# Moving bias rows, cache loads, cache transposes and one weight split to other places in a hybrid-attention step

## The chip, the cores and the metric

The kernel runs on one core of a Trainium2 chip. The metric is device time in microseconds (us) of one execution; lower is better. Times of the kernel before come from three runs (median 970.5 us, 969.71 to 972.78) and from one execution that was also profiled (969.89 us).

## The reference

The program is one inference step (one layer) of a streaming encoder, for a prompt of 1024 rows and a sample of 64 rows of 1024 numbers, in float32:

```
def project(x, norm_w, w_in, q_norm_w, k_norm_w):
    h = rms_norm(x, norm_w) @ w_in
    sb_q, sb_k, sb_v, sb_z, cb_q, cb_k, cb_v, cb_z, g_sb, g_cb = jnp.split(h, SPLIT_POINTS, axis=-1)
    ...
    cb_q = rms_norm(cb_q.reshape(lead + (N_HEADS_CB, HEAD_DIM)), q_norm_w)
    cb_k = rms_norm(cb_k.reshape(lead + (N_HEADS_CB, HEAD_DIM)), k_norm_w)

def merge(x, o_sb, z_sb, o_cb, z_cb, g_sb, g_cb, w_proj_sb, w_proj_cb, w_out):
    b_sb = (o_sb.reshape(lead + (WIDTH_SB,)) * jax.nn.silu(z_sb)) @ w_proj_sb
    b_cb = (o_cb.reshape(lead + (WIDTH_CB,)) * jax.nn.silu(z_cb)) @ w_proj_cb
    h = jax.nn.sigmoid(g_sb) * b_sb + jax.nn.sigmoid(g_cb) * b_cb
    return x + h @ w_out
```

Between the two stand a stick-breaking attention (sb, 8 heads of 64) and a chunk-band attention (cb, 8 heads of 64) with a bias that depends on the clipped relative position. The sample rows attend to 512 cached keys and values of each kind as well (`cache_sb_k`, `cache_cb_k`, 512 x 512 each). What matters here is the projection `x @ w_in` and what is prepared beside it for the attention: the cached keys, turned so that a head's 64 numbers lie along the partitions, and rows of the bias laid out per relative position.

## The kernel before, in words

**How the work is written.** Every engine has its own instruction stream, which it works off in order; the schedule is manual, so the order of the streams is the order of the source. A tile of a pool has a fixed number of buffers, and whoever writes a buffer again waits for its last readers. TensorE (PE in the profile) multiplies and transposes, ScalarE (ACT) and VectorE (DVE) empty its accumulators, GpSimd (POOL) subtracts and raises to powers, and SyncE (SP) issues nearly all DMAs in one queue, in order: a DMA that waits for its source or its buffer holds up all that stand behind it. Float32 products are made from two fp32r halves: `hi` is a rounded copy made on ScalarE, `lo` the difference from it, made on POOL or VectorE; one product takes three matmuls (hi x hi, lo x hi, hi x lo).

**First stage: six passes of nine tiles.** The loop `for i in range(nb)` runs over six column blocks of 256 columns of `w_in`, and within it `for ti, t in enumerate(TO)` over nine row tiles: the sample tile first (ti = 0, 64 rows, 16 matmuls), then eight prompt tiles (ti = 1 to 8, 24 matmuls each). I write (i, ti) for a place in it. After the matmuls of a place, in the order of the source:

- `post_nat` transposes an earlier tile's normalised result on PE into `pk`, which ScalarE and VectorE copy out as `hl` (lines 370 to 375). `pk` has one buffer.
- `evac_nat` empties the accumulator: ScalarE squares it (`sqn`, L340), VectorE scales and reduces it (`qn`, `msn`, L341, L343), POOL makes the reciprocal root (`rsn`, L272, L273). For the sample tile `fold` comes first, one copy on ScalarE (`fl`, L318) and one addition on VectorE (L319).
- `norm_nat` scales the tile before on ScalarE (`qn`, L352, four instructions).
- At ti = 3 and ti = 6 `W.split` makes the halves of the next pass's weights (ScalarE L131, then POOL L138 `wlo` or `wlox`), and `load_nat` issues the load of the weights of the pass after that (L123, `wraw` or `wrawx`). `wrawx` has one buffer, so its load waits for POOL's `wlox`.
- At some places `make_rb(h)` makes the bias row of head h on VectorE (`rx`, L267 and L268, two buffers) from the bias table, which sits in a tile named `ck`, and sends it to DRAM (L269).
- At eight places `next(tjobs)` adds up four pieces of x on VectorE (`d`, L189), and splits the sum of the job before into `t0h`, `t0l` and so on (ScalarE L172, VectorE L173).
- `cache_load(b)` loads one cache's keys, 1024 KB, into the tile `ck` (L386). `ck` has one buffer, shared by the bias table, the sb keys and the cb keys in turn.
- `cache_pair(b, p)` turns a quarter of them: four transposes on PE into `pc` (L392; one buffer, PSUM), a copy on ScalarE into `hc` (L394; one buffer), the difference on VectorE (L395), and a DMA of `hc` to DRAM (`d_csbT`, `d_ccbT`, L52).

Before the change `make_rb` runs at every second place from (1, 0) to (2, 5); the sb cache is loaded at (2, 6) and turned at (3, 1), (3, 3), (3, 5), (3, 7); the cb cache is loaded at (3, 7) and turned at (4, 1), (4, 3), (4, 5), (4, 7).

**Second stage: seven products.** The loop `for s in range(7)` makes the cb values of the prompt from seven products of sums of x and sums of weight blocks instead of eight. Each step s has 48 matmuls (L699), half for c = 0 and half for c = 1, and `split_quad` makes the halves of a weight sum for a later step: that of `quad[0, 0]`, which holds a difference of weight blocks, is made at s = 2 on ScalarE and VectorE (`whix` L474, `wlox` L476) and used at s = 4. The sixteen jobs of `tjobs` must be through by s = 5; the last three are called at (s, c) = (0, 0), (0, 1), (1, 0). The results gather in three banks of two: step 1 fills bank 2, step 4 adds to it, step 5 adds again. So PE may start a half of step 4 only when VectorE has read bank 2 after step 1 (`u`, L707), and a half of step 5 only when VectorE has read it after step 4 (`o`, L714). `o` has two buffers; step 3 sends two of them to DRAM (`put_v`, L635), and step 4 writes the same buffers. Ahead of those DMAs in SP's queue stand the ones of the sample's result (`fl`, L319 on VectorE, L653 to L655).

After these stages come the other columns of the projection (L863), the attention (L1032 to L1380) and the output.

Of the kernel before, what the change touches and what calls it, by code (L numbers as in the profile page):

```python
# [33 lines left out]
def hybrid_step_kernel(ctx: ExitStack, tc: tile.TileContext, x_prompt, x_sample, c_sbk, c_sbv, c_cbk, c_cbv,  # L34
# [58 lines left out]
    def pad(pool, n):  # L93
        pool.tile([128, n // 4], F32, name=f"pad{n}", bufs=1)
# [119 lines left out]
    with ExitStack() as ph:  # L214
# [49 lines left out]
        def make_rb(h):  # L264
            rb = rbs[0]
            rx = p1h.tile([128, 768], F32, name="rx", bufs=2)
            V.tensor_scalar(rx[:, 0:512], rb[:, h, 256:257].to_broadcast([128, 512]), -1.0, None, op0=OP.mult)  # L267
            V.tensor_scalar(rx[:, 512:768], rb[:, h, 255::-1], -1.0, None, op0=OP.mult)  # L268
            SP.dma_start(d_rb[h], rx)  # L269
# [259 lines left out]
        tms = [None] * 4  # L529
        jobs_at = [(2, 0), (2, 3), (2, 6), (3, 0), (3, 4), (3, 7), (4, 1), (4, 4)]  # L530

        def open_t(ns):
            tp = sx.enter_context(tc.tile_pool(name=f"tp{ns[0]}", bufs=1, side="right"))
            for n in ns:
                tms[n] = [tp.tile([128, 4, XO], F32R, name=f"t{n}{s}") for s in "hl"]
            if ns[0] == 0:
                pad(tp, 128)

        for i in range(nb):
            if i == 1:  # L540
                p0x.close()
                open_t((0, 1))
                tjobs = make_t(tms, tq)
            for ti, t in enumerate(TO):
# [28 lines left out]
                if i == 0:  # L573
                    if ti == 2:
                        load_nat(1, 0)
                        load_nat(1, 1)
                        SP.dma_start(wqk[:, 0], q_norm_w[0:1, :].to_broadcast([128, 64]))
                        SP.dma_start(wqk[:, 1], k_norm_w[0:1, :].to_broadcast([128, 64]))
                if ti in (3, 6) and i > 0 or ti in (6, 7) and i == 0:
                    h = 1 if ti == (6 if i else 7) else 0  # L580
                    if i + 1 < nb:
                        W.split((i + 1, h), V if i == 0 and h else None)
                    if i + 2 < nb:
                        load_nat(i + 2, h)
                    elif i + 2 == nb:
                        load_quad(h, 0, *((natx, "wrawx", 1) if h else (wpool, "wraw", 2)))
                if (i, ti) == (0, 4):
                    load_rb()
                if (9 * i + ti - 9) % 2 == 0 and 0 <= 9 * i + ti - 9 < 16:
                    make_rb((9 * i + ti - 9) // 2)  # L590
                if i == nb - 1 and ti == 1:
                    load_quad(0, 1, wpool, "wraw", 2)
                    load_quad(1, 1, pn, "q11", 1)
# [17 lines left out]
                    V.tensor_tensor(out=quad[0, 0], in0=quad[0, 0], in1=quad[0, 1], op=OP.subtract)  # L611
                if (i, ti) in jobs_at or i == nb - 1 and ti >= 4:
                    next(tjobs)
                if (i, ti) in ((2, 6), (3, 7)):
                    cache_load("sb" if i == 2 else "cb")
                if i in (3, 4) and ti in (1, 3, 5, 7):
                    cache_pair("sb" if i == 3 else "cb", ti // 2)
                if (i, ti) in ((1, 1), (1, 5)):
                    for s in range(2):
                        h = ti // 4  # L620
# [42 lines left out]
        for s in range(7):  # L663
# [27 lines left out]
            for c in range(2):  # L691
                if s < 3:
                    bank["1231223"[s], c] = psB.tile([128, 512], F32, name=f"b{'1231223'[s]}{c}")
                ps = bank["1231223"[s], c]
                for tt in range(2):
                    o = ps[:, 256 * tt:256 * tt + 256]
                    for k in range(4):
                        for e, (xe, w) in enumerate(((0, wh), (1, wh), (0, wl))):
                            TE.matmul(o, x(xe, k, 2 * c + tt), w[:, k], start=s < 3 and k == e == tt == 0,  # L699
                                      stop=k == 3 and e == 2, skip_group_check=True)  # L700
                two = lambda v: (v[:, 0:256], v[:, 256:512])
                if s == 0:
                    s1[c] = nu.tile([128, 512], F32, name="s1")
                    A.activation(s1[c], ps, AF.Copy)
                elif s == 1:
                    u2[c] = nu.tile([128, 512], F32, name="u2")
                    V.tensor_tensor(out=u2[c], in0=ps, in1=s1[c], op=OP.add)  # L707
                elif s == 3:
                    v = nu.tile([128, 512], F32, name="o")
                    A.activation(v, ps, AF.Copy)  # L710
                    put_v(0, 0, c, two(v))
                elif s == 4:
                    v = nu.tile([128, 512], F32, name="o")
                    V.tensor_tensor(out=v, in0=ps, in1=s1[c], op=OP.add)  # L714
                    V.tensor_tensor(out=v, in0=bank["3", c], in1=v, op=OP.add)
                    put_v(1, 1, c, two(v))
                elif s == 5:
                    V.tensor_tensor(out=s1[c], in0=ps, in1=s1[c], op=OP.add)
                    put_v(1, 0, c, two(s1[c]))
                elif s == 6:  # L720
                    V.tensor_tensor(out=u2[c], in0=ps, in1=u2[c], op=OP.add)
                    put_v(0, 1, c, two(u2[c]))
                if 2 * s + c < 3:
                    next(tjobs)
        assert not list(tjobs)

# [1066 lines left out]
```

## Time and profile before

| what | value |
|---|---|
| median of three runs | 970.5 us (969.71 to 972.78) |
| the profiled execution's own time | 969.89 us |
| its span, from the first to the last instruction | 968.1 us |
| mean granted clock of TensorE | 0.995 |
| TensorE busy | 954.5 us, 99% of the span |
| VectorE, ScalarE, POOL busy | 590.5, 500.4, 394.4 us |

All times below count from the span's start. First-stage passes 2, 3 and 4 lie between 67 and 159 us, the second stage between 181 and 228 us. The chain that ended last gives TensorE 89% of the span. A matmul's row shows the start of it and a modelled end; the distance between starts (some 0.12 us for 256 columns at full clock) is what it costs. In a timeline row the first two numbers are start and duration in us; a bracket at the end names the idle time before the instruction and what released it. In a row of windows stand, after the stretch, its length, then the busy time of PE, of the weight loads (PEld), DVE, ACT and POOL with the instructions in brackets, the granted clock of TensorE, the share of the DMA engines and GB/s.

### The profile page before, as it was taken

The page shows a single profiled execution, that of the slowest core. Times are in us where ns is not written, and L with a number is a line of the kernel's source. Part 1 is how long each engine was busy: PE and PEld are TensorE (multiplying, and loading weights), DVE is VectorE, ACT ScalarE, POOL GpSimd, SP SyncE. Part 2 cuts the span into 40 slices and gives each one's busy share as a digit, 9 for nine tenths or more (in the row PEclk, how much of TensorE's full clock was granted, in tenths as well). Part 3 has the DMA queues.
Part 4 walks back from the last instruction along what each step waited for, and adds up shares of the span by engine and source line. Part 5 has one row for each costly group of instructions (what it writes and reads, how often), then busy time and mean ns, then how long its engine had stood idle before and what let it go on. Part 6 is the DMA issues. An engine that isn't in the chain of part 4 may idle for free.

```text
span 968.1 us, 20544 instructions
## 1 busy us (share of the span) xinstructions
PE 954.5 (99%) x7595; PEld 907.2 (94%) x7595; DVE 590.5 (61%) x1156; ACT 500.4 (52%) x1159; POOL 394.4 (41%) x393
## 2 busy tenths in 40 slices
PE   9999899999999999999999999999999999999998
PEld 8999899989999999999999987788888988999998
DVE  6656564984454555534322298777777865499745
ACT  6566575332434433333342377667886874466220
POOL 3277464335444556665542200011331111686641
PEclk9999999999999999999999999999999999999999
DMA  7745666325646565555523997679799833852742
GB/s 226 245 130 195 221 223 227 111 71 192 190 142 184 171 189 169 170 173 152 179 86 103 283 244 211 161 189 250 237 296 252 243 108 89 255 176 84 219 139 75
DMA packets 173498, 175.77 MB, mean 182 GB/s; under 512 B 30922, under 2 KB 157710, under 8 KB 173271
## 3 DMA queue, kind: packets, MB, share of 16 engines
q1 hardware_dynamic: 162102, 159.58, 55.5%
q10 hardware_dynamic: 8608, 8.20, 2.7%
q0 software_dynamic: 2688, 6.69, 2.1%
q8 instruction: 60, 0.98, 0.4%
q14 instruction: 40, 0.32, 0.1%
HBM read 112.42 MB, written 62.00 MB: 180 GB/s over the span
## 4 chain that ended last, share of the span: by engine, by line
PE 89%; DVE 5%; DMA 2%; ACT 1%; issue 1%; POOL 1%; ACTq 0%; DVEq 0%; SPq 0%; POOLq 0%
PE b L863 30%; PE acc L528 13%; PE o L1380 7%; PE z L1288 7%; PE pt L1341 7%; PE b L1700 6%; PE acc L1139 5%; PE acc L1032 5%; PE b L1181 4%; PE b L699 2%; DVE d L189 2%; PE pt L301 1%; DMA ck<-in_cache_sb_k_dram 1%; DMA ck<-in_cache_cb_k_dram 1%; DVE acc L1226 1%
## 5 line engine op out<-in xcount | busy, mean ns | idle before, releaser
L1310 DVE TENSOR_TENSOR_SCAN be<-be,imp 128x128 f32<-128x128 f32 (+7 forms) x64 | 83.4, 1343 | 8.1 <-ACT be L1291 7.9
L1341 PE MATMUL pt<-ident,be 128*128 128x128 f32 (+1 forms) x568 | 87.7, 278 | 0.6 <-ACT wT L1350 0.4
L1288 PE MATMUL z<-ks,sq 128*128 128x320 f32 (+5 forms) x384 | 87.5, 338 | 0.0
L1350 ACT ACTIVATE wT<-pt 128x512 f32<-128x512 f32 (+3 forms) x123 | 57.0, 496 | 42.9 <-PE pt L1341 42.8
L1341 PEld LDWEIGHTS pt<-ident,be 128*128 128x128 f32 (+1 forms) x568 | 65.7, 140 | 13.1 <-issue 4.6
L863 PE MATMUL b<-xm,wlox 128*128 128x256 f32 (+1 forms) x336 | 76.0, 286 | 0.0
L871 DVE TENSOR_TENSOR u<-b,s 128x256 f32<-128x256 f32 (+1 forms) x56 | 24.4, 440 | 75.5 <-PE b L863 71.1
L1288 PEld LDWEIGHTS z<-ks,sq 128*128 128x128 f32 x384 | 63.7, 190 | 1.7
L1380 PE MATMUL o<-wT,vp 128*64 128x256 f32 (+1 forms) x608 | 64.2, 356 | 0.0
L1380 PEld LDWEIGHTS o<-wT,vp 128*64 128x64 f32 x608 | 40.3, 136 | 23.6 <-issue 7.5
L863 PEld LDWEIGHTS b<-xm,wlox 128*128 128x128 f32 x336 | 56.8, 188 | 0.0
L1313 ACT ACTIVATE be<-be,sm 128x640 f32<-128x640 f32 (+5 forms) x68 | 47.2, 695 | 17.2 <-DVE sm L1312 17.2
L528 PE MATMUL acc<-whi,xa 128*128 128x256 f32 x192 | 53.1, 296 | 0.0
L936 POOL DMA_DIRECT2D d_osb<-zt x20 | 10.8, 541 | 101.6 <-DVE zt L1389 55.3
L528 PE MATMUL acc<-wlo,xa 128*128 128x256 f32 x192 | 50.2, 281 | 0.0
L528 PE MATMUL acc<-whi,xm 128*128 128x256 f32 x192 | 50.2, 281 | 0.0
L528 PE MATMUL acc<-whix,xm 128*128 128x256 f32 x192 | 50.1, 280 | 0.0
L528 PE MATMUL acc<-whix,xb 128*128 128x256 f32 x192 | 50.1, 280 | 0.0
L528 PE MATMUL acc<-wlox,xm 128*128 128x256 f32 x192 | 49.9, 280 | 0.0
L1301 ACT ACTIVATE be<-be,sm 128x640 f32<-128x640 f32 (+5 forms) x68 | 47.3, 696 | 4.9 <-DVE sm L1293 4.5
L457 POOL TENSOR_TENSOR whix<-ws,whix 128x512 fp32r<-128x512 f32 x28 | 36.6, 1307 | 31.9 <-ACT whix L456 25.7
L1291 ACT ACTIVATE be<-z 128x384 f32<-128x384 f32 (+6 forms) x104 | 47.9, 515 | 3.2 <-PE z L1288 2.3
(379 smaller groups left out, 3256.6 us busy)
## 6 DMA issues: line engine op xcount, KB each, us to landing
wraw<-in_w_in_dram SPq DMA_DIRECT2D x31, 512.0 KB, 4.6
wrawx<-in_w_in_dram SPq DMA_DIRECT2D x16, 512.0 KB, 4.9
sq<-d_qsbT SPq DMA_DIRECT2D x32, 192.0 KB, 6.2
sq<-d_qcbT SPq DMA_DIRECT2D x32, 192.0 KB, 5.5
xt<-in_x_prompt_dram SPq DMA_DIRECT2D x8, 512.0 KB
d_kcbT<-hl SPq DMA_DIRECT2D x8, 512.0 KB
d_qcbT<-hl SPq DMA_DIRECT2D x8, 512.0 KB, 5.4
ks<-d_ksbT SPq DMA_DIRECT2D x16, 256.0 KB, 6.1
```

Source lines behind the costliest of these rows:

```text
L528: TE.matmul(ps, x, w, start=first, stop=last)
L863: TE.matmul(ps[:, :m], w[:, hl_, k], right[s](x)[:, k, a:b], start=s < 3 and k == 0 and e == 0, stop=k == 3 and e == 2, skip_group_check=s ...
L1032: TE.matmul(ps[:, :b - a], w[:, k], xk(x, k)[:, a:b], start=k == 0 and n == 0, stop=k == KT - 1 and n == 2)
L1139: TE.matmul(ps[:, :e - a], w[:, p, cw], g[:, a:e], start=m % 12 == 0, stop=m % 12 == 11)
L1288: TE.matmul(z[:, :m], s[:, e, q0:q0 + 128], ks[:, h, o + x:o + y], start=(e, h) == parts[0], stop=(e, h) == parts[-1])
L1291: A.activation(be[:r, x:y], z[:r, :m], AF.Sigmoid, scale=-0.125)
L1301: A.activation(be[:, :n], be[:, :n], AF.Exp, bias=kp[:, j:j + 1], scale=-1.0, accum_out=kp[:, 2:3])
L1310: V.tensor_tensor_scan(be[:r, n - 1::-1], be[:r, n - 1::-1], im[:, ::-1], 0.0, op0=OP.mult, op1=OP.max)
L1341: TE.transpose(pt[:kr, x, :r], be[:r, kb * 128:kb * 128 + kr], ident[:r, :r])
L1350: A.activation(w[:, sl:sl + m, q0:q0 + r], pt[:, :m, :r], AF.Copy)
L1380: TE.matmul(o[hd * 64:hd * 64 + 64, c0:c1], vv[:kr, kb, hd * 64:hd * 64 + 64], wT[b, p, j, hd, s // 4][:kr, s % 4, c0:c1] if j < 4 else wT ...
L1700: TE.matmul(ps[:, t], left[s](xs_, k)[:, ts_], wt_[:, k], start=s < 3 and t == k == e == 0, stop=k == 3 and e == 2, skip_group_check=s > 2 ...
```

## The change

Three things move, and no instruction is added or removed.

- Bias rows: `make_rb` runs at (1, 0), (1, 1), (1, 3), (1, 4), (1, 6), (1, 7), (2, 0), (2, 1), so the last is four places earlier than before.
- Caches: `cache_load` is called at (2, 2) for sb and (3, 2) for cb, in the source ahead of the weight loads at ti = 3 and 6. The sb keys are turned at (2, 5), (2, 7), (3, 0), (3, 1) and the cb keys at (3, 5), (3, 7), (4, 0), (4, 1).
- The last of the sixteen jobs is called at (s, c) = (2, 0) in place of (1, 0), and so stands behind the split of `quad[0, 0]`.

```
+        rb_at = [(1, 0), (1, 1), (1, 3), (1, 4), (1, 6), (1, 7), (2, 0), (2, 1)]
...
+                if ti == 2 and i in (2, 3):
+                    cache_load("sb" if i == 2 else "cb")
                 if ti in (3, 6) and i > 0 or ti in (6, 7) and i == 0:
...
-                if (9 * i + ti - 9) % 2 == 0 and 0 <= 9 * i + ti - 9 < 16:
-                    make_rb((9 * i + ti - 9) // 2)
+                if (i, ti) in rb_at:
+                    make_rb(rb_at.index((i, ti)))
...
-                if (i, ti) in ((2, 6), (3, 7)):
-                    cache_load("sb" if i == 2 else "cb")
-                if i in (3, 4) and ti in (1, 3, 5, 7):
-                    cache_pair("sb" if i == 3 else "cb", ti // 2)
+                at = [(2, 5), (2, 7), (3, 0), (3, 1)]
+                if (i, ti) in at:
+                    cache_pair("sb", at.index((i, ti)))
+                if (i - 1, ti) in at:
+                    cache_pair("cb", at.index((i - 1, ti)))
...
-                if 2 * s + c < 3:
+                if (s, c) in ((0, 0), (0, 1), (2, 0)):
                     next(tjobs)
```

What this does to the streams is seen at three places. The first is SP's queue in pass 2: `d_rb` are the bias rows, `ck` the cache load, `wraw` and `wrawx` the weight loads at ti = 3 and ti = 6, `d_csbT_78` the first turned quarter of the sb keys, `out_dram` and `d_kcbT` results of pass 2 and pass 1.

```order
-L269 DMA d_rb_131<-rx 128x768
+L269 DMA d_rb_133<-rx 128x768
+L386 DMA ck<-in_cache_sb_k_dram 128x4x512
 L52 DMA d_kcbT_74<-hl 256x1x512
 L52 DMA d_kcbT_75<-hl 256x1x512
 L123 DMA wraw<-in_w_in_dram 128x4x256
-L269 DMA d_rb_132<-rx 128x768
-L269 DMA d_rb_133<-rx 128x768
+L52 DMA d_csbT_78<-hc 128x1024
 L357 DMA out_dram<-qn 128x256
 L123 DMA wrawx<-in_w_in_dram 128x4x256
-L386 DMA ck<-in_cache_sb_k_dram 128x4x512
```

The cache load moved from behind both weight loads to ahead of both, right behind the last bias row. The second place is ScalarE at (3, 0) and (3, 1), from the sample's `fold` on, before the change:

```order
L318 ACTIVATE fl<-acc 64x256
L340 ACTIVATE sqn<-fl 64x256
L352 ACTIVATE qn<-qn,rsn 128x64 x4
L172 ACTIVATE t0h<-d 128x544
L374 ACTIVATE hl<-pk 128x2x128
L340 ACTIVATE sqn<-acc 128x256
L352 ACTIVATE qn<-qn,rsn 64x64 x4
L394 ACTIVATE hc<-pc 128x512
```

And the same place after the change, where the two rows of `hc` are the third and the fourth quarter of the sb keys (before, the one row was the first quarter):

```order
L318 ACTIVATE fl<-acc 64x256
L340 ACTIVATE sqn<-fl 64x256
L352 ACTIVATE qn<-qn,rsn 128x64 x4
L172 ACTIVATE t0h<-d 128x544
L394 ACTIVATE hc<-pc 128x512
L374 ACTIVATE hl<-pk 128x2x128
L340 ACTIVATE sqn<-acc 128x256
L352 ACTIVATE qn<-qn,rsn 64x64 x4
L394 ACTIVATE hc<-pc 128x512
```

Two quarters now follow each other one place apart, the first of them behind the sample's `fold` and a job's `t0h`. The third place is VectorE in the second stage, around the last job (`d` and `t3l`), the two reads of bank 2 after step 1 (`u`) and the split for step 4 (`wlox`):

```order
-L707 TENSOR_TENSOR u_2960<-b_2935,s_2890 128x512
+L712 TENSOR_TENSOR u_2960<-b_2935,s_2890 128x512
+L712 TENSOR_TENSOR u_2987<-b_2962,s_2923 128x512
+L476 TENSOR_TENSOR wlox<-wraw,whix 128x1024
 L189 TENSOR_TENSOR d<-xm,t1h 128x544
 L189 TENSOR_TENSOR d<-d,xb 128x544
 L189 TENSOR_TENSOR d<-d,t1l 128x544
 L173 TENSOR_TENSOR t3l<-d,t3h 128x544 x2
-L707 TENSOR_TENSOR u_2995<-b_2970,s_2923 128x512
-L476 TENSOR_TENSOR wlox<-wraw,whix 128x1024
-L673 TENSOR_TENSOR s_2758<-wrawx,s_2758 128x1024
+L678 TENSOR_TENSOR s_2758<-wrawx,s_2758 128x1024
```

The split and the second read of bank 2 moved ahead of the last job; the instructions from the first `u` to `s` are the same ones in another order. On ScalarE the split's `whix` moved ahead of the last two `t3h` likewise.

## The prediction

> **What bounds the kernel now.** I read the page first, for which engine is full, then TensorE's waits, then the windows around each wait.
>
> ```profile
> span 968.1 us, 20544 instructions
> PE 954.5 (99%) x7595; PEld 907.2 (94%) x7595; DVE 590.5 (61%) x1156; ACT 500.4 (52%) x1159; POOL 394.4 (41%) x393
> ```
>
> TensorE is full. A reordering can win only what TensorE waits, and what waiting does to its clock. The waits of TensorE, longest in total:
>
> ```profile
> PE pc L392 <- DMA ck<-in_cache_sb_k_dram: 3.2, 1, 3.2
> ...
> PE pc L392 <- DMA ck<-in_cache_cb_k_dram: 1.4, 1, 1.4
> PE b L699 <- DVE wlox L476: 1.0, 1, 1.0
> PE b L699 <- ACT whix L474: 0.9, 1, 0.9
> ```
>
> These four are what the change aims at: 3.2 + 1.4 + 1.0 + 0.9 = 6.5 us. Next, the windows that hold each wait and the ones behind them; the number to see is the granted clock, third from the end:
>
> ```profile
> 99.20:102.50 3.30, 0.66 (x6) 0.66 (x7) 2.35 (x6) 2.08 (x7) 2.21 (x4) 1.00 0.96 335
> 102.60:105.80 3.20, 3.20 (x18) 3.20 (x17) 0.69 (x1) 0.53 (x1) 0.44 (x1) 0.51 1.11 395
> 129.80:133.20 3.40, 2.33 (x20) 2.09 (x19) 2.00 (x6) 2.52 (x10) 2.00 (x3) 1.00 1.00 302
> 133.30:136.60 3.30, 3.12 (x27) 3.12 (x28) 3.23 (x7) 1.63 (x5) 2.02 (x2) 1.00 1.03 380
> 204.90:208.30 3.40, 1.52 (x11) 1.12 (x10) 3.31 (x6) 3.04 (x5) 0.46 (x1) 1.00 0.00 0
> 208.40:211.70 3.30, 3.28 (x15) 3.28 (x16) 3.30 (x2) 0.88 (x2) 2.20 (x1) 0.51 0.54 159
> ```
>
> Where TensorE worked 0.66 of 3.3 us or 1.52 of 3.4 us, the next 3.3 us ran at half clock; where it worked 2.33 of 3.4, nothing followed. So between 1.1 and 1.9 us of idleness in such a stretch the clock falls. The price is in the chain, whose rows are start, duration, what:
>
> ```profile
> 102.50 4.34 PE acc L528 x24
> 107.06 2.75 PE acc L528 x24
> ...
> 216.59 11.12 PE b L699 x96
> ```
>
> The tile after the sb wait took 4.34 us, a tile at full clock 2.75: 1.6 us lost. Two of three places paid it, so the most that can be won is 6.5 + 2 x 1.6 = 9.7 us.
>
> **The bias rows and the sb load.** SP's queue, VectorE's last two bias-row instructions at (2, 1), and TensorE after the matmuls of (2, 5), (3, 1) and (4, 1):
>
> ```profile
> 94.04 0.38 SPq L123 DMA_DIRECT2D wrawx<-in_w_in_dram  x1
> 94.47 0.50 SPq L386 DMA_DIRECT2D ck<-in_cache_sb_k_dram  x1
> 113.85 0.53 SPq L52 DMA_DIRECT2D d_csbT<-hc  x1
> 128.28 0.34 SPq L52 DMA_DIRECT2D d_csbT<-hc  x1
> 74.37 0.42 DVE L267 TENSOR_SCALAR rx<-ck 128x512 f32<-128x512 f32 x1
> 74.70 0.29 DVE L268 TENSOR_SCALAR rx<-ck 128x256 f32<-128x256 f32 x1
> 84.09 0.38 PE L370 MATMUL pk<-ident,qn 128*128 128x128 f32 x2
> 98.22 0.38 PE L370 MATMUL pk<-ident,qn 128*128 128x128 f32 x2
> 131.75 0.38 PE L370 MATMUL pk<-ident,qn 128*128 128x128 f32 x2
> ```
>
> The load was issued at 94.47, behind `wrawx`, and landed when the wait of 3.2 us ended, 98.6 + 3.2 = 101.8: 7.3 us. Now it waits only for the last bias row. At (2, 1) a row is made at 74.37 to 74.99 already; one more at (2, 0) pushes it by 0.7, to 75.7. With SP's time for the row's DMA the load goes out at about 76.3 and lands at 83.6. The first transposes can start behind `pk` at 84.09, at 84.3. That wait is gone, with 0.7 us to spare; I take 0, and up to 0.7 for the range, since a bias row may itself wait for its buffer's DMA.
>
> The eight bias rows cost VectorE what they did, 0.7 us each; two in neighbouring places delay `hl` by as much, and `pk` has its place of 3 us to cover it. Nothing on the path.
>
> **What is late next at (3, 1).** The quarters are now at (2, 5), (2, 7), (3, 0) and (3, 1), and `pc` and `hc` have one buffer each. So the transposes of the fourth wait for ScalarE and VectorE to be through with the third, which stands behind the sample's `fold` and a job:
>
> ```profile
> 97.96 1.05 ACT L352 ACTIVATE qn<-qn,rsn 128x64 f32<-128x64 f32 x4
> 98.92 0.64 ACT L172 ACTIVATE t0h<-d 128x544 fp32r<-128x544 f32 x1
> 102.53 0.60 ACT L394 ACTIVATE hc<-pc 128x512 fp32r<-128x512 f32 x1 [0.61 <-PE pc L392]
> 119.55 0.60 ACT L394 ACTIVATE hc<-pc 128x512 fp32r<-128x512 f32 x1 [0.87 <-DMA d_csbT<-hc]
> 130.72 1.06 ACT L352 ACTIVATE qn<-qn,rsn 128x64 f32<-128x64 f32 x4
> 134.79 0.60 ACT L394 ACTIVATE hc<-pc 128x512 fp32r<-128x512 f32 x1 [0.46 <-DMA d_csbT<-hc]
> 99.88 0.72 DVE L173 TENSOR_TENSOR t0l<-d,t0h 128x544 fp32r<-128x544 f32 x1
> 103.16 0.69 DVE L395 TENSOR_TENSOR hc<-pc,hc 128x512 fp32r<-128x512 f32 x1 [1.57 <-ACT hc L394]
> ```
>
> Four transposes cost TensorE 0.45 us (0.41 from 101.84 to the next product, which began at 102.25). Three sets ahead of (3, 1) move its end from 98.22 by 1.35 to 99.6, so the fourth set could start at 99.8. The third `hc` on ScalarE: `t0h` ended at 99.56, and ScalarE is pushed by 0.45, since it waits there for POOL, which is one set later: 100.0 to 100.6. On VectorE `t0l`, 99.88 to 100.60, also moves by 0.45, to 101.05; then `hc` takes 0.69: 101.75. TensorE waits from 99.8 to 101.75: 1.9 us in place of 3.2. The tile behind it starts at 102.2, as before; the gain comes later, when the three sets no longer stand in (3, 3), (3, 5), (3, 7): 3.2 - 1.9 = 1.3 us.
>
> The DMA of the second quarter also decides: `hc` can be written only when it has landed. It stands behind `wrawx` (94.04, now 94.5) and goes out at 95.4. Landings seen here are 119.55 - 113.85 = 5.7 us and, behind a whole cache load, 134.79 - 128.28 = 6.5, and I take 4.5, as only `wrawx` and a small result are ahead: 99.9, just in time. At 6.5 it is 101.9.
>
> **The cb load and (4, 1).** The cb load is issued behind the fourth sb quarter's DMA, whose `hc` waits for the third's landing (101.8 + about 3): it goes out near 106.2, lands 7.3 later at 113.5, and is wanted after (3, 5), near 114.2. I take 0, with 0.7 for the range. The chain at (4, 0) has no job: ScalarE's `qn` ends at 130.72 + 1.06 = 131.8, `hc` 0.60 and 0.69 later at 133.1. TensorE could start the fourth cb set at 131.75 + 0.45 + 0.25 = 132.45. A wait of 0.65 in place of 1.4: 0.75 us won.
>
> **The second stage.** VectorE from the first `u` on, POOL and ScalarE for step 5's weights, and the last sample matmul before step 4:
>
> ```profile
> 202.35 0.68 DVE L707 TENSOR_TENSOR u<-b,s 128x512 f32<-128x512 f32 x1
> 207.15 1.22 DVE L476 TENSOR_TENSOR wlox<-wraw,whix 128x1024 fp32r<-128x1024 f32 x1
> 208.28 3.40 DVE L673 TENSOR_TENSOR s<-wrawx,s 128x1024 f32<-128x1024 f32 x1
> 211.60 0.41 DVE L319 TENSOR_TENSOR fl<-acc,fl 64x256 f32<-64x256 f32 x1
> 215.78 0.69 DVE L714 TENSOR_TENSOR o<-b,s 128x512 f32<-128x512 f32 x1 [3.77 <-DMA d_cbv<-o]
> 207.84 2.76 POOL L476 TENSOR_TENSOR wlo<-q,whi 128x1024 fp32r<-128x1024 f32 x1 [6.63 <-ACT whi L474]
> 206.72 1.04 ACT L474 ACTIVATE whi<-q 128x1024 fp32r<-128x1024 f32 x1
> 205.64 0.28 PE L649 MATMUL acc<-wlo,xs 128*128 128x256 f32 x1
> ```
>
> Two `u` from 202.35 and then `wlox` end at 202.35 + 0.65 + 0.65 + 1.15 = 204.8. TensorE comes to step 4 at 205.76, so both waits (1.0 and 0.9) and their clock loss go: step 4's 48 matmuls at 0.116 (11.12 / 96) end near 211.2 and the eight of the sample at 212.1, where before they ended at 216.4.
>
> But step 5 adds to bank 2, which `o` (L714) must have read, and that instruction waited 3.77 us for the DMAs of the `o` buffers, which stand in SP's queue behind those of `fl`. So its time hangs on VectorE's `fl`. The stretch from 202.35 to `s` holds the same work, and `s` starts at 208.3 in both. Before, POOL had begun `wlo` at 207.84 and `s` took 3.40 us, done 1.1 after POOL ended at 210.6. Now `whi<-q` stands behind a later `t3h`, ends at 208.6 rather than 207.76, and POOL comes at 208.7, when `s` has begun: 1.2 us, to 209.5. `fl` follows to 209.9, `o` starts 3.77 later at 213.65 and ends at 214.3. POOL's `wlo`, behind `s`, takes 2.4 and is there at 211.9, 0.7 after the sample's matmuls want it. Step 5 starts at 214.3 in place of 216.5: 2.2 us won out of the 3.5 that the wait and the clock cost. The section on who interferes with whom in the Trainium skill's page SBUF — State Buffer says that the engine that comes first keeps the shared port for its whole instruction and the other is blocked; the 3.40 us of `s` agrees with it.
>
> **The sum.** 1.3 + 0.75 + 2.2 = 4.25 us from waits, and the clock: before, 1.6 us were lost at (3, 2), and those of the second stage are in the 2.2. TensorE now has two new gaps long enough to matter: 1.9 us at (3, 1), and 0.7 + 1.4 = 2.1 us in 3 us at step 5. If the stretches that decide fall at random against a gap of 2 us, at least 1.5 of it lies in one of them in about 6 of 10 cases. Of two gaps one most likely costs 1.6: 1.6 back and 1.6 lost. So 4.25 us, from 969.9 to 965.6 of the profiled execution. That execution was 0.6 below the median of the three runs, so 970.5 - 4.25 = 966.2, my forecast. Behind 228 us TensorE stays full, and an earlier start is an earlier end.
>
> **Rivals.** (a) Neither gap costs clock: 1.6 more, 964.6. The section Why this matters for your kernels of the Trainium skill's page TensorE: Matmul & The Clock Gate says that gaps up to about 3 us are harmless; against it stands the window 204.90:208.30, 1.9 us idle, half clock after. It could still come so by the stretches' position. Chance 0.2, with one gap 0.35, with both (967.8) 0.15.
> (b) All waits go and nothing replaces them, 9.7 us: 970.5 - 9.7 = 960.8. For it, the loads are early; against it, one `pc` and one `hc`. Chance 0.07.
> (c) Step 5 takes the whole of the second stage's gain: POOL begins `wlo` before `s`, so `s` takes 3.4 us again and `fl` and `o` come as late as before. The margin is 208.7 - 208.3 = 0.4 us. Then 2.2 is gone: 968.4. Chance 0.13.
> (d) Slower: the second quarter's DMA lands late. From 6.5 us on (seen once), `hc` starts at 101.9, `pc` is free at 103.3, and TensorE waits 3.5 us and loses the clock, as much as before. The third DMA then goes out at 103.3 and lands at 109.8, ScalarE stands from 103 to 109.8 before the fourth `hc`, `pk` at (3, 3) and (3, 4) waits some 2 us for its `hl`, the cb load goes out at 111.5 and lands at 118.8, against 116 wanted: 2.8 us and 1.6 of clock. With the same at (4, 1), 2 us more than before: 2 + 4.4 + 2 - 2.2 = 6 us longer, 976; half of it, at 5.7 us, is 972. For it, 5.7 and 6.5 were seen; against it, both behind more bytes than now. Chance 0.1.
> That the change does nothing cannot be: the queue is another.
>
> **Numbers.** 966.2; cases (a) to (c) lie from 960.8 to 968.4. The range 962.0 to 969.5 leaves out (b) and most of (d), and holds the unknown 0.7 us twice. A measurement of this kernel can tell about 0.3%, 2.9 us, from no change: faster is below 967.6, (a), the forecast, (b) and some of the both-gaps case: 0.66. Same, the rest of that and (c), and part of (d): 0.25. Slower 0.09.
>
> **What would show it.** Right: no wait for either `ck` DMA; waits of `pc` for VectorE's `hc` (L395) of 1.9 and 0.65 us; no wait of L699 for L474 or L476, but one of 1 to 2 us for `o` at step 5; a bias row ended by 76; half clock behind at most one or two gaps. Wrong: a wait for `ck` that stays; ScalarE standing over 3 us for `d_csbT`; `s` taking 3.4 us; a total under 962 or over 969.5.

## The result and the profile after

| | before | after |
|---|---|---|
| median of five runs each | 970.84 us (969.71 to 972.78) | 966.19 us (964.74 to 967.78) |
| ratio of after to before, 95% interval | | 0.995 (0.9933 to 0.9967) |
| the profiled execution's own time | 969.89 us | 966.22 us |
| its span | 968.1 us | 964.4 us |
| its mean granted clock | 0.995 | 1.000 |

The change takes 4.65 us, and the forecast was 4.25 us, to 966.2. That the times agree so closely is partly luck: the gain was 0.4 us larger and the median before 0.3 us higher than the forecast took them. In the terms, as the section on why it was right shows, the waits behaved much as forecast, the clock better, and a part of the kernel that the change doesn't touch ran slower in the profiled execution.

The page's row of the engines' busy time, after:

```profile
PE 952.6 (99%) x7595; PEld 905.4 (94%) x7595; DVE 587.8 (61%) x1156; ACT 499.9 (52%) x1159; POOL 393.3 (41%) x393
```

TensorE is busy 1.9 us less and idle 1.8 us less. Its waits after the change at the places that it touches (total, times, longest, in us):

```profile
PE pc L392 <- DVE hc L395: 2.9, 2, 2.2
...
PE b L704 <- DVE o L719: 1.3, 1, 1.3
```

The four waits of 6.5 us that the change aims at are gone. In their place stand two for `hc`, 2.24 and 0.70 us, and one for `o`. The windows at (3, 1) and behind it, where the granted clock is the third number from the end:

```profile
99.20:102.50 3.30, 1.16 (x11) 0.92 (x9) 3.04 (x6) 2.67 (x10) 2.08 (x2) 1.00 1.05 395
102.60:105.90 3.30, 3.30 (x29) 3.30 (x30) 0.93 (x3) 0.70 (x3) 1.20 (x2) 1.00 0.80 290
```

TensorE stands for 2.1 of 3.3 us, but the window behind it is at full clock. (Why 2.1 us cost nothing here is answered below, under the question whether idleness halves the clock.) The rows of SP, ScalarE, VectorE, TensorE and POOL that answer to the steps of the prediction, first those around (3, 1), the last three from the second stage:

```profile
76.94 0.43 SPq L386 DMA_DIRECT2D ck<-in_cache_sb_k_dram  x1
96.09 0.38 SPq L52 DMA_DIRECT2D d_csbT<-hc  x1
107.94 0.39 SPq L386 DMA_DIRECT2D ck<-in_cache_cb_k_dram  x1
101.22 0.60 ACT L394 ACTIVATE hc<-pc 128x512 fp32r<-128x512 f32 x1 [0.63 <-DMA d_csbT<-hc]
101.85 0.69 DVE L395 TENSOR_TENSOR hc<-pc,hc 128x512 fp32r<-128x512 f32 x1 [0.22 <-ACT hc L394]
102.60 0.66 PE L392 MATMUL pc<-ident,ck 128*128 128x128 f32 x4 [2.24 <-DVE hc L395]
205.47 1.22 DVE L678 TENSOR_TENSOR s<-wrawx,s 128x1024 f32<-128x1024 f32 x1
205.82 3.13 POOL L476 TENSOR_TENSOR wlo<-q,whi 128x1024 fp32r<-128x1024 f32 x1 [7.42 <-ACT whi L474]
210.77 0.69 DVE L719 TENSOR_TENSOR o<-b,s 128x512 f32<-128x512 f32 x1 [3.76 <-DMA d_cbv<-o]
```

Three landmarks date the gain: the start of step 5, the long stretch of other columns that starts 85 us later, and a group of 48 matmuls in the last stage. From the chain that ended last, before:

```profile
301.76 223.42 PE b L863 x1800
952.27 5.44 PE b L1700 x48
```

and after, with step 5 on the first line:

```profile
211.51 11.17 PE b L704 x96
296.97 223.46 PE b L868 x1800
948.11 5.65 PE b L1705 x48
```

Step 5 starts 216.59 - 211.51 = 5.1 us earlier, the long stretch 4.8 us earlier. The last two rows differ by only 952.27 - 948.11 = 4.2 us, and the spans by 3.7: these groups of 48 matmuls in the last stage take 5.65 instead of 5.44 us.

### The profile page after: what moved, and what is told of

The parts are those of the page before. It is cut to its first block, busy times and chain, and to the rows that moved or that the text cites. A ratio compares the mean times of both kernels' runs of the same rounds, so it can differ in the third digit from the quotient of the medians.

```text
span 964.4 us, 20547 instructions
## 1 busy us (share of the span) xinstructions
PE 952.6 (99%) x7595; PEld 905.4 (94%) x7595; DVE 587.8 (61%) x1156; ACT 499.9 (52%) x1159; POOL 393.3 (41%) x393
## 4 chain that ended last, share of the span: by engine, by line
PE 91%; DVE 5%; DMA 2%; ACT 2%; issue 1%; SPq 0%; POOL 0%; DVEq 0%; ACTq 0%
PE b L868 30%; PE acc L528 12%; PE b L1705 8%; PE o L1385 7%; PE z L1293 7%; PE pt L1346 7%; PE acc L1144 5%; PE b L1186 5%; PE acc L1037 5%; DVE d L189 2%; PE b L704 1%; PE pt L301 1%; PE pk L370 1%; PE acc L787 1%; PE acc L1748 1%
```

## The experiments

Twelve kernels were run. Where I speak of a start of the long stretch, it is the row of 1800 matmuls in the chain: 301.76 before, 296.97 after. The profiled executions differ before any edit acts: TensorE starts pass 1 at 41.63 us before, at 41.92 after, and between 41.38 and 42.03 in all fourteen profiles. Where it matters I give a start with this difference taken off as well, and call it corrected.

**The two halves of the change apart.** First the second stage alone: before, with only the last job moved.

```
-                if 2 * s + c < 3:
+                if (s, c) in ((0, 0), (0, 1), (2, 0)):
                     next(tjobs)
```

> The kernel before with only the last job moved behind the split of quad[0, 0]. Theory (the two parts add up): the waits of L699 for whix (0.9) and wlox (1.0) and the half clock behind them go, step 5 then waits 1.3 to 1.4 us for o, the wait for both ck loads stays at 3.2 and 1.4; 2.2 us less than before, 968.6. Rival (the wait only moves to step 5): o is as late as before, no change, 970.8, and s takes 3.4 us beside POOL again.

Measured: 968.48 us against 970.61, ratio 0.9972 (0.9959 to 0.9985). Its waits:

```profile
PE pc L392 <- DMA ck<-in_cache_sb_k_dram: 3.3, 1, 3.3
PE pc L392 <- DMA ck<-in_cache_cb_k_dram: 1.6, 1, 1.6
```

The waits for `whix` and `wlox` are gone, one of 1.4 us for `o` has come, and those for `ck` stand about as before, with the half clock behind the first. The long stretch starts at 299.88, 1.9 us earlier. The second stage is worth some 2 us, as forecast (2.2).

Then the first stage alone: the change with the job back at (1, 0).

```
-                if (s, c) in ((0, 0), (0, 1), (2, 0)):
+                if 2 * s + c < 3:
                     next(tjobs)
```

> The changed kernel with the last job back at (1, 0): bias rows and caches alone. Theory: both waits for ck go, pc waits 2.2 and 0.7 us for hc instead, the half clock after (3, 1) goes, and the waits of step 4 stay with theirs; 3.1 us less than before, 967.7. Rival (the whole gain is made here): 966.2.

Measured: 968.21 us, ratio 0.9959 (0.9943 to 0.9975). Two of its waits:

```profile
PE pc L392 <- DVE hc L395: 3.1, 2, 2.4
...
PE b L704 <- DVE wlox L476: 1.0, 1, 1.0
```

The waits for `hc` are about those of the change and `wlox` is waited for again. No half clock followed it in this execution, and step 5 then waited 1.7 us for `o`, which before it didn't: part of what a full clock gives at step 4 is lost again at step 5. The long stretch starts at 299.05, 2.7 us earlier than before (3.1 corrected). 1.9 + 2.7 = 4.6, and the whole change moves it by 4.8 (corrected, 1.9 + 3.1 = 5.0 and 5.1): the halves add up as far as one profile of each can tell.

**What the wait for `hc` hangs on.** Theory: the fourth set of transposes finds the one buffer of `pc` held by the third, so a second buffer frees it. The change with two buffers of `pc`:

```
-            pt = psK.tile([128, 4, 128], F32, name="pc")
+            pt = psK.tile([128, 4, 128], F32, name="pc", bufs=2)
```

> The changed kernel with two buffers of pc. Theory: the fourth set of transposes no longer waits for VectorE to be through with the third, so both waits of pc (2.2 and 0.7 us) go and nothing takes their place: 2.9 less than the changed kernel, 963.3. Rival: ScalarE, still held before hc by the one buffer of hc and its DMA, is late with hl, and pk waits instead: 965 to 966.

Measured: 964.52 us (962.92 to 968.35), ratio 0.9933 (0.9912 to 0.9953), between the theory and the rival. Its longest wait, now that those for `hc` no longer stand:

```profile
PE pk L370 <- DVE hl L375: 2.2, 3, 1.6
```

and ScalarE's row for the fourth quarter, which `hl` stands behind:

```profile
106.13 0.60 ACT L394 ACTIVATE hc<-pc 128x512 fp32r<-128x512 f32 x1 [2.86 <-DMA d_csbT<-hc]
106.63 0.38 ACT L374 ACTIVATE hl<-pk 128x256 fp32r<-128x256 f32 x1
```

The wait moved rather than went: ScalarE stands 2.86 us until the third quarter's DMA has left the one buffer of `hc`, and `hl` behind it holds `pk`. So the bottleneck is the chain of single buffers from `pc` through `hc` to its DMA. If so, a second `hc` as well should free all of it:

```
-            h = p1.tile([128, 2, 512], F32R, name="hc", bufs=1)
+            h = p1.tile([128, 2, 512], F32R, name="hc", bufs=2)
```

> The change with two buffers of pc and two of hc. Theory, the single hc (its DMA must land before ScalarE may write it again) is what made pk wait 2.2 us when pc alone was doubled: with both doubled neither pc nor pk waits, 2.9 us less than the change, about 963.3, and 1.2 to 2 us less than with pc alone. Rival, ScalarE is late at (3, 1) for its own work (the sample's fold, a job): pk still waits 1.5 us or more and the time is that of pc alone, 964.5.

Measured: 962.09 us against 969.71, ratio 0.9916 (0.9896 to 0.9935). What is left of the waits there:

```profile
PE pk L370 <- DVE hl L375: 0.3, 1, 0.3
PE pc L392 <- DMA ck<-in_cache_cb_k_dram: 0.2, 1, 0.2
```

No wait of `pc` or `pk` is over 0.3 us, and ScalarE isn't late by its own work: the rival falls. The other way to the same end needs no buffer, only distance. The change with the quarters apart:

```
-                if ti == 2 and i in (2, 3):
+                if (i, ti) in ((2, 2), (3, 4)):
                     cache_load("sb" if i == 2 else "cb")
...
-                at = [(2, 5), (2, 7), (3, 0), (3, 1)]
+                at = [(2, 5), (2, 7), (3, 1), (3, 3)]
+                cat = [(3, 7), (4, 1), (4, 3), (4, 5)]
```

> The change with its quarters moved apart, still one buffer each of pc and hc: sb at (2, 5), (2, 7), (3, 1), (3, 3); cb loaded at (3, 4) and turned at (3, 7), (4, 1), (4, 3), (4, 5). Theory, the waits for pc at (3, 1) and (4, 1) come from two quarters one place apart: both go (2.2 + 0.7 us in the profile of the change), no wait of pk takes their place since each hc's DMA has two places to land, and the time is 2.9 us less than the change, about 963.3; the second part of the attention starts about 294.1 instead of 296.97 us. Rival, the third quarter behind the sample tile's work is what is late, not the distance: a wait of 1 to 2 us stays. Second rival, the cb load, now two places later, is late for (3, 7): a wait for ck of 1 us or more and about 965.

Measured: 962.23 us, ratio 0.9916 (0.9897 to 0.9936). From its chain:

```profile
207.64 11.15 PE b L705 x96
292.85 223.42 PE b L869 x1800
```

No wait for `hc`, `ck` or `hl` is over 0.3 us, and the long stretch starts at 292.85, 4.1 us earlier than after the change. The waits for `hc` had been 2.9; its execution was 0.3 us ahead from the start, and the rest I didn't trace. One buffer each is enough when the quarters stand two places apart.

**The rival on the slower side.** The prediction's rival (d) needs the second quarter's DMA to land late. To make it so, an extra copy that nobody reads goes out just ahead of it:

```
+                if (i, ti) == (2, 7):
+                    SP.dma_start(d_x, c_cbv)
```

> The change with an extra copy of 1024 KB from DRAM to DRAM (the cb value cache into a scratch that nobody reads) in SP's queue just ahead of the second sb quarter's DMA at (2, 7). This makes that DMA land late, which is my rival on the slower side. Theory of that rival: landing some 3 us later than the 5.1 us of the change, ScalarE's third hc waits for it, the wait of pc at (3, 1) grows from 2.2 to about 5 us, half clock behind it costs 1.6, ScalarE stands 3 us or more ahead of the fourth hc and pk waits for its hl some 1 to 2 us: 5 to 6 us longer than the change, 971 to 972. Rival, the landing does not depend on what is ahead in the queue, or the place has cover: no change, 966.2.

Measured: 973.47 us (969.88 to 975.74), slower than before: ratio 1.0036 (1.0022 to 1.0051). SP issued the quarter's DMA at 96.77, and ScalarE's rows for the third and fourth quarter are

```profile
104.50 0.60 ACT L395 ACTIVATE hc<-pc 128x512 fp32r<-128x512 f32 x1 [3.89 <-DMA d_csbT<-hc]
109.47 0.60 ACT L395 ACTIVATE hc<-pc 128x512 fp32r<-128x512 f32 x1 [2.89 <-DMA d_csbT<-hc]
```

The DMA landed after 104.50 - 96.77 = 7.7 us instead of 5.1. TensorE's wait at (3, 1) and the tile behind it, from the waits and from the chain:

```profile
PE pc L393 <- DVE hc L396: 6.2, 2, 5.5
...
PE pk L371 <- DVE hl L376: 0.4, 1, 0.4
```

```profile
106.99 4.83 PE acc L529 x24
...
302.51 223.41 PE b L871 x1800
```

5.5 us of wait and 4.83 - 2.75 = 2.1 us of half clock, as the rival says, and the long stretch starts 5.5 us later than after the change. The wait of `pk` that the rival added (2 us) didn't come (0.4 in all): ScalarE was through with the fourth quarter at 110.1, and TensorE's slow tile lasted to 106.99 + 4.83 = 111.8. Nor did its wait for a late cb load (2.8 us): no wait for `ck` over 0.2 us is left. (The cb quarters weren't made late here, so what it says of (4, 1) is not tested.) So the rival was a true mechanism with some of its terms too large, and the change stood 2.6 us of landing time away from a large part of it.

**What step 5 waits for.** The prediction put it on the DMAs that must leave `o`. Step 4's results in another tile:

```
                 elif s == 4:
-                    v = nu.tile([128, 512], F32, name="o")
+                    v = made[1][:].rearrange("p k n -> p (k n)")[:, 512 * c:512 * c + 512]
```

> The changed kernel with the results of step 4 written to a tile that is free by then in place of the two buffers of o, so that they no longer wait for the DMAs of step 3. Theory: the wait of step 5 for o (1.3 us) goes and the rest stays: 964.9. Rival: step 5 is then held by POOL's wlo for the sample's product or by the next DMA, no change, 966.2.

Measured: 966.74 us, ratio 0.9962 (0.9942 to 0.9981), no gain over the change. Yet step 5 did start earlier, at 210.01 instead of 211.51 (1.0 us corrected), without a wait for `o`. The chain behind it shows where that went:

```profile
210.01 10.90 PE b L704 x96
...
227.76 0.45 SPq L410
...
228.32 4.66 DMA wraw<-in_w_in_dram
...
233.10 1.03 DVE ws L422
...
237.49 0.55 PE acc L787 x3
```

SP issues the stores of the second stage one after the other, and the next stage's weight loads (L410) stand behind them. They land at 233.0, VectorE makes `ws` from them, and TensorE waits at L787 (0.8 us in all); the long stretch starts at 296.78, 0.2 earlier and, corrected, 0.3 later. This edit brought part of the delay itself, since `made[1]` was also the room of the next stage's `ws`: VectorE's first `ws` stood 6.58 us until the stores from there had left, which after the change it didn't. A cleaner test leaves the buffers alone and moves only the queue: the three DMAs of the sample's `fl` go behind those of step 3's results.

```
                 v = fold(pn, ps)
...
-                SP.dma_start(d_cbv[0:32, n], v[0:32])
-                SP.dma_start(d_cbv[NP + 32:T, n], v[32:64])
-                SP.dma_start(o_cbv_s[32:64, n], v[32:64])
+                def out():
+                    SP.dma_start(d_cbv[0:32, n], v[0:32])
+                    SP.dma_start(d_cbv[NP + 32:T, n], v[32:64])
+                    SP.dma_start(o_cbv_s[32:64, n], v[32:64])
+                if w:
+                    out()
+                else:
+                    held.append(out)
...
                     put_v(0, 0, c, two(v))
+                    if c:
+                        held.pop()()
```

> The change with the three DMAs of the sample's first result (fl, after step 3) put into SP's queue behind those of step 3's two results instead of ahead of them. Theory, step 5 waits 1.3 us because the DMAs of o stand in SP's queue behind fl, which VectorE makes late: the first o leaves when ScalarE has made it, about 206.8 instead of 208.41 us, the wait for o at step 5 goes, step 5 starts 1.3 us or more earlier (210.2 or sooner), and since SP's queue is not made longer the third stage keeps it: the second part of the other columns starts about 295.6 instead of 296.97, 964.9 against 966.2. Rival, as with step 4's results in another tile: the third stage takes it back (its loads behind the stores), step 5 is earlier and the total is not, 966.2. Second rival, o leaves as late as before for its own reason: the wait stays.

Measured: 965.57 us, ratio 0.9947 (0.9927 to 0.9968): in the total not to be told from the change. In its profile VectorE's row for `o`, and from the chain the sample's matmuls ahead of step 5 and the long stretch:

```profile
209.37 0.69 DVE L727 TENSOR_TENSOR o<-b,s 128x512 f32<-128x512 f32 x1 [2.18 <-DMA d_cbv<-o]
```

```profile
209.49 0.91 PE acc L654 x8
...
295.38 223.47 PE b L876 x1800
```

`o` comes at 209.37 instead of 210.77, TensorE goes from the sample's matmuls into step 5 at 210.40 without waiting, and the long stretch starts 1.6 us earlier (1.3 corrected, the wait's own length): the queue was the cause, and here the next stage keeps the gain in the profile. Together with the quarters apart:

> The quarters moved apart (run above) and the sample's three DMAs behind those of step 3's results, together. Theory, the two are independent: 962.2 less 1.3, about 960.9, the second part of the other columns starts about 291.5. Rival, the third stage takes the second gain back: 962.2, start at 292.8.

Measured: 959.92 us (958.55 to 961.0) against 970.91, ratio 0.9887 (0.9866 to 0.9908): the fastest of all, 0.6% below the change. Its two longest waits, which lie at the start of the program and in the attention, and its long stretch:

```profile
PE pc L484 <- POOL half L255: 1.4, 1, 1.4
PE pt L1355 <- ACT wT L1364: 0.4, 2, 0.2
```

```profile
291.58 223.42 PE b L877 x1800
```

No wait at the places of the prediction is left among them, and 292.85 - 291.58 = 1.3 us (1.7 corrected) are the second edit's share.

**Is it idleness that halves the clock?** Before, with extra matmuls of the identity into `pc` while TensorE waits for the sb load; the next transposes overwrite what they write.

```
             pt = psK.tile([128, 4, 128], F32, name="pc")
+            for t in range(20 if (b, p) == ("sb", 0) else 0):
+                TE.matmul(pt[:, t % 4], ident, ident, start=True, stop=True)
```

> Before, with twenty extra matmuls of the identity into `pc` ahead of the first sb quarter, so that TensorE works while it waits for the sb load at (3, 1); their result is overwritten. They need no `ck`, so they lie inside the wait of 3.2 us (20 at about 0.1 us, some 2 us). Theory, the clock falls because TensorE idles: the load still ends the wait at the same time, but the next 24 matmuls take 2.75 us instead of 4.34, so everything behind starts 1.6 us earlier; about 969.2 against 970.8, and the last stages start 1.6 us earlier in the chain. Rival, the clock falls at that place for another reason: half clock stays and the time is that of before, 970.8. Second rival, the matmuls do not fit into the wait: up to 2 us longer.

Measured: 968.13 us against 969.71, ratio 0.998 (0.9966 to 0.9994). The extra matmuls and the tile behind them, from its chain:

```profile
98.84 4.47 PE pc L392 x40
...
103.75 2.73 PE acc L530 x24
```

The clock part of the theory holds: 2.73 us in place of 4.34. But the matmuls were twice as dear as I had taken them (each is a pair on TensorE, 4.47 / 20 = 0.22 us) and overran the wait, so the tile was over at 106.48 instead of 106.84, and the wait for the cb load took that back in this profile (1.6 instead of 1.4); the long stretch starts at 301.91 (0.1 earlier corrected). The median of the twelve executions, 1.6 us below before, is what the theory forecast all the same. Hence eight of them:

> Before, with eight instead of twenty extra matmuls in the wait for the sb load; each took 0.22 us in the run with twenty, so eight are 1.8 us and end about 100.3, inside the wait, which ends at 101.8 with 1.5 us of idleness left. Theory, a gap under about 1.9 us in a stretch costs no clock: the window behind shows 1.00, the next 24 matmuls take 2.75 instead of 4.34, the next tile starts at about 105.5 instead of 107.06 us, and the second part of the other columns 1.6 us earlier or less, where the cb load or step 4 take some back; about 968.2 against 969.7. Rival, any gap over 1 us costs it: half clock stays, 969.7.

Measured: 969.38 us, ratio 0.9988 (0.9973 to 1.0004). Its wait and, from the chain, the tile behind it:

```profile
PE pc L394 <- DMA ck<-in_cache_sb_k_dram: 2.4, 1, 2.4
```

```profile
103.21 4.36 PE acc L530 x24
```

A gap of 2.4 us was left, not 1.5, since the load landed later, and in this execution it cost the same as the whole 3.2 us. That is neither the theory's gap nor the rival's proof. So twelve:

> Before, with twelve extra matmuls in the wait for the sb load. In the run with eight they took 1.95 us from 98.2 and left 2.42 us of idleness, behind which the half clock came as before; with twenty they filled the wait and overran it by some 1.2 us, and no half clock came. Twelve take 2.9 us, end at 101.1 and leave 1.4 to 1.5 us. Theory, half clock comes only when most of a stretch of some 3.3 us is idle: none here, the next 24 matmuls take 2.75 us instead of 4.34, the tile after them starts at about 105.4 instead of 107.06, and the second part of the other columns 1.6 us earlier (300.1 instead of 301.76) unless the cb load's wait takes back up to 0.4; about 0.998 of before. Rival, any gap over 1 us costs it: half clock as in before and a ratio of 1.

Measured: 968.73 us, ratio 0.9986 (0.9973 to 0.9999). The extra matmuls and the first transposes on TensorE, then the tile behind them and the cb load from the chain:

```profile
98.80 2.84 PE L392 MATMUL pc<-ident 128*128 128x128 f32 x24
102.28 0.66 PE L394 MATMUL pc<-ident,ck 128*128 128x128 f32 x4 [0.64 <-DMA ck<-in_cache_sb_k_dram]
```

```profile
102.94 2.83 PE acc L530 x24
...
124.98 8.28 DMA ck<-in_cache_cb_k_dram
```

With 0.64 us of gap there is no half clock, and the next tile starts at 105.98 instead of 107.06. But the cb load, issued 1.2 us earlier than before's 126.18, landed at 133.3 all the same (8.28 us instead of 7.26), and the wait for it grew to 2.5. That wait cost half clock in turn: the tile behind it, at 133.96, took 4.35 us. The profiled execution lost more further on (2.6 us for `o`, and stalls in the last stage) and took 971.3 us of span where most of its others took 967, so its later rows I don't use. The gap of 1.4 us that I wanted was not met. The runs show that idleness brings the half clock. What filling the wait is worth in time they show less well: with twenty extra matmuls 1.6 us (0.998, interval 0.9966 to 0.9994), with eight and twelve 1.2 and 1.4 us, with intervals that reach 1 or just miss it.

**How much idleness, and where.** The granted clock in the traces settles this. In all fourteen, half clock comes in stretches of 3.41 us (twice that in the run with the late DMA), and the stretches of one execution lie on one grid of that step: before, they begin at 102.65 and 208.46, 31 steps apart, and again at 966.22, 222 steps on, when TensorE has nothing left to do. So I laid the windows on that grid; where no stretch at half clock came earlier, the one behind the last matmul places it. First the gap of 2.6 us of the run with `fl`'s DMAs moved, then the one of 2.4 us of the run with eight matmuls, then the gap of 2.4 us of the run with the first stage alone:

```profile
98.25:101.66 3.41, 1.86 (x17) 1.63 (x15) 2.96 (x6) 2.26 (x7) 2.08 (x2) 1.00 1.06 402
101.66:105.08 3.42, 2.38 (x20) 2.38 (x21) 1.68 (x4) 1.74 (x7) 1.20 (x2) 1.00 0.97 360
```

```profile
100.45:103.87 3.42, 1.31 (x11) 1.31 (x12) 0.89 (x3) 1.66 (x5) 1.32 (x3) 1.00 1.07 394
103.87:107.28 3.41, 3.41 (x18) 3.41 (x17) 0.69 (x1) 0.00 (x0) 0.00 (x0) 0.50 0.74 267
```

```profile
101.06:104.48 3.42, 1.61 (x14) 1.62 (x15) 2.39 (x6) 2.08 (x7) 1.38 (x3) 1.00 1.09 387
```

The grid cuts the gap of 2.6 us into 1.55 and 1.04 us, and no half clock follows; 2.11 us of the gap in the run with eight matmuls lie in one stretch, and the next one is at half clock. Of the third, 1.80 us lie in one stretch, and the next is at full clock. So it is over all fourteen traces, up to TensorE's last matmul: nine stretches at full clock hold 1.98 to 3.41 us of idleness, and half clock follows each; all the others hold 1.80 us or less, and it follows none. (The late DMA's second stretch at half clock follows one that was itself at half clock and held 1.38 us.) The ends of matmuls are modelled, so the bound, between 1.80 and 1.98 us of idleness in one stretch of 3.41, is good to perhaps 0.1 us. Whether a gap costs thus depends on how the grid lies over it, and that differs from execution to execution.

## Why the prediction was right

**The loads.** The last bias row ended at 76.5 (forecast 76) and the sb load went out at 76.94 (76.3); TensorE never waited for it. The cb load went out at 107.94, 1.7 us later than forecast, and was still in time. Rightly taken at 0.

**The waits that replace them.** The forecast was 1.9 us at (3, 1) and 0.65 at (4, 1); the trace has 2.24 and 0.70. The first is longer because the second quarter's DMA was not "just in time": it took 5.1 us instead of the 4.5 that I chose between no row and 5.7, and held ScalarE by 0.63 us. Only 0.22 us of this reach TensorE, for so long VectorE stood for ScalarE's `hc`; until then it had been at `t0l` itself, later than I had reckoned. So the step gave 3.2 - 2.2 = 1.0 instead of 1.3. That the single buffers are the cause is shown: with two of each, or with the quarters apart, both waits are gone.

**The second stage.** Forecast 2.2 us. Of the 5.1 us at step 5's start, 1.0 and 0.7 are the two waits, 1.6 the tile behind (3, 1), and the execution after the change was 0.3 us later from the start (pass 1 at 41.92 instead of 41.63). That leaves 5.1 + 0.3 - 1.0 - 0.7 - 1.6 = 2.1 for the second stage; the run with that half alone gave 1.9. `s` began 0.35 us ahead of POOL and took 1.22 us (forecast 0.4 and 1.2), `o` waited 3.76 us for its DMA (3.77), TensorE 1.30 (1.4); the 0.7 us that the sample's matmuls were to wait for POOL's `wlo` didn't come, since it was done at 208.95, ahead of them. Rival (c), POOL first, failed by that 0.35 us.

**The clock: the step that failed.** "Of two gaps one most likely costs 1.6" didn't hold. In the profiled execution both windows behind the gaps are at 1.00, which was rival (a). Over many executions it can be counted: a stretch of 3.41 us at half clock loses 1.7 us and takes 0.0018 from an execution's mean granted clock, while the idle end of the program takes up to 0.001 and costs nothing. So a mean of 0.999 or more says no such stretch, 0.998 and 0.997 say one, 0.996 and 0.995 two, 0.994 three. The five executions of the change (1.000, 0.997, 0.999, 1.000, 0.999) have one among them, 0.3 us on average where the forecast had 1.6. The 77 of before in four comparisons have 1.5 each, 2.6 us where the forecast had 3.2. So a little over 2 us came back where the forecast had 1.6. Five executions are few: the change, its first stage alone, and the runs with step 4's results elsewhere and with `fl`'s DMAs moved all have the wait of 2.2 to 2.6 us at (3, 1), and of their 28 executions 11 show one stretch and none two. With the waits for `hc` gone (both buffers doubled, the quarters apart, both edits) none of 17 does; with the late DMA all ten show two or more. And filling the wait with twenty matmuls brings it down from 1.3 to 0.6 stretches an execution in the same comparison.

The step behind it was the rule of 1.5 us idle in a stretch. It was right in kind, "the stretches that decide" lie on a grid that falls at random against a gap, and too low in size: it takes between 1.80 and 1.98 us. By the prediction's own working a gap of 2 us has 1.5 of it in one stretch in 7 of 10 cases (it says 6); with 1.9 us the gap of 2.24 us comes to 1 - (2 x 1.9 - 2.24) / 3.41, about half, as an estimate from these figures. After the change the grid cut it into 1.56 and 0.68 us. The Trainium skill's page TensorE: Matmul & The Clock Gate, section Why this matters for your kernels, holds gaps up to about 3 us harmless. The gaps of 2.24 us here, 2.4 in the run with the first stage alone and 2.6 in the run with `fl`'s DMAs moved agree; the 2.4 us in the run with eight matmuls and, before, 1.9 us in two gaps don't, since the grid left 2.11 and 2.00 us of them in one stretch.

**The total.** At the start of the long stretch the gain was 4.8 us in the profile pair, and 1.2 more came at 880 to 905 us, so that the same group of 48 matmuls starts 903.95 - 897.93 = 6.0 us earlier. Those 1.2 us aren't the change's: the runs with twenty and with eight extra matmuls, which hold nothing of it, gain 1.5 and 1.3 us on before between the long stretch and the group at 910.57 (909.18 and 910.56 in them). The profiled execution before lost them there. Then 2.3 us were lost in the last 66 us: 64.15 us before, 66.47 after, at a clock granted in full in both while TensorE works. So the profiled pair shows 3.7 us and the medians 4.65; the mechanism was right, the clock's term too small by 1.6 us in the pair and by some 0.6 us over the executions, the wait at (3, 1) too short by 0.3, and the rest is the spread of executions. The sum of 4.25 was closer than its terms.

## What to carry to other kernels

Before moving a producer earlier, follow its buffers to the end: a PSUM tile, its copy and the copy's DMA, with one buffer each, need as much distance between two uses as the DMA takes to land, and doubling only the first of them moves the wait instead of removing it. When a wait goes, look at the queue that feeds the next stage, because a gain that doesn't also bring that queue's loads forward is given back there. Price the clock by its average over several executions, not by what one profile shows: here a gap cost 1.7 us only where the grid of 3.41 us left some 1.9 us or more of it in one stretch, so the same gap cost it in one execution and not in the next.

## What was not expected of the hardware

- Matmuls ran at two paces at a full granted clock. Groups of 48 near the end of the last stage (from about 905 us on) took 5.44 us in the profiles of seven of the fourteen kernels here and 5.65 in the other seven, 4% apart and worth 2.3 us over the last 66 us. The rows at 952.27 before and at 948.11 after are one of each. The pace can change within an execution: after the change, the first four groups of this stage still took 5.44 (two rows of 96 matmuls, 10.91 and 10.88 us), up to 897.9. What sets the pace, no run here tells.
- TensorE's clock was granted in steps of 3.41 us on a grid that lay differently in each execution. Of the steps at full clock, the nine with TensorE busy for 1.43 us or less were followed by one at half clock, all those with 1.61 us or more by one at full clock. A gap of 2.6 us therefore cost nothing in one execution and one of 2.4 us at the same place cost 1.6 us in another.
- A transfer that was issued 1.2 us earlier landed no earlier (the cb load above): its time of landing hung on something other than its place in the queue.
